# Small products of a modulation vector and of a block merge, streamed with 128 columns instead of 1 and 32

## The chip, the cores and the metric

The kernel runs on one core of a Trainium2 chip. The metric is the device time of one execution in microseconds (us); less is better. Before the change three runs gave 1183.56, 1184.01 and 1186.36 us, median 1184.01.

## The reference

One residual block of a streaming encoder on a sequence of 1024 tokens of width 1024, all in float32:

```python
mod = (c_act @ w_ada[l] + b_ada[l])[:, None, :]          # c_act = silu(c), one vector
shift1, scale1, gate1, shift2, scale2, gate2 = jnp.split(mod, 6, axis=-1)
h = rms_norm(x, norm1_w[l]) * (1.0 + scale1) + shift1
x = x + gate1 * hybrid_mixer(h, ...)     # p = h @ w_in; gated delta rule + short conv; @ w_out
h = rms_norm(x, norm2_w[l]) * (1.0 + scale2) + shift2
x = x + gate2 * swiglu(h, ...)
return rms_norm(x, norm_f_w)
```

Two pieces matter here. The first is the product of the vector `c_act` with the first two column blocks of `w_ada`, which gives `shift1` and `scale1`. The second lies in the gated delta rule: for each head and each chunk of 64 tokens a unit lower triangular 64x64 matrix `lmat` is inverted (`tmat`), and `u = tmat @ v_beta` and `w = tmat @ (k_beta * exp(g))` follow.

## The kernel before, in words

TensorE multiplies 128x128 weights (loaded by a LDWEIGHTS record) with a moving operand of up to 512 columns into one of eight PSUM banks of 128x512. The dense projections split float32 operands into two parts of type float32r and multiply these (128x512 products, one record each; in the profile `acc`, `dn`, `o`). Smaller products take plain float32 operands, and each such product appears as two records, each with a weight load of its own.

The first half of the program (to about 480 us) is not issued in the order in which it is written. Tasks run as threads under a planner (`Sim`, line 298), which keeps an estimated clock for each engine, picks the next operation by priority and estimated start, and so writes out a fixed order for each engine; `Sim.either` (line 438) makes the call, so nearly every operation of this half has line 442 in the profile. Each engine then runs its own list strictly in order and waits on semaphores. The planner's price of a float32 product is `max(n * 0.00168, 0.224)` us for `n` columns (in `Sim.cost`), so 1, 32 and 128 columns all cost it 0.224.

The stages that the change touches:

- Start (to about 54 us). PE first multiplies `ones` by `ident` a number of times into a bank called `heat` whose content nobody reads (line 240 and `acc0`, line 679). `ada0` (line 625) forms `shift1` and `scale1` for eight groups `k` of 128 channels, in one bank (`ada`). Weights are the 128x128 blocks of `w_ada`, and the moving operand is one column of `c_act`. The result of a product is one column, two columns for each group. `sums0` on VectorE (DVE) has summed up most blocks of groups 1 to 7 beforehand, into `ac`; for these a product of `ac` with a column of `ones` does the sum over partitions. `cols0` (line 646, ScalarE, ACT) reads the two columns and makes from them the scale and shift of that group (`s1c`, `b1c`), which `h_make` uses. There are 38 products, 76 records.
- The merge of the delta rule, once for each half of the sequence (`hf` 0 at 202 us, `hf` 1 at 390 us). DVE solves the 32x32 diagonal blocks by substitution (in `gdn`, line 1218); they go to DRAM and come back as `DD`, `xbd` and `XA`. For each of four heads `merge` (line 1178) multiplies twice with 32 moving columns: `P` = weights `L` times a 32-column block of `DD`; ACT copies `P` back into `DD`; `Q` = weights `XA` times that. Four copies of 32x64 place `Q` into `Tt`, the inverse of the 64x64 blocks. Then come the products `u` (weights `Tt`, 128 moving columns) and `w` (128 columns). For each half there are 8 products `P` and 8 `Q`, that is 16 records each. PE's list has all `P`, one `acc` record, all `Q`, and then `u` and `w` with single `acc` records between them.

`bc1(row, n)` (line 140) gives a view with an axis of `n` repeats and step 0; `tsl(t)` (line 1074) is the slice of columns `128*t` to `128*t+128`; `v3(ap, a)` views columns as `a` groups; `mm` (line 581) is one matmul.

Of the kernel before, what the change touches and what calls it, by code (L numbers as in the profile page):

```python
# [12 lines left out]
AF = mybir.ActivationFunctionType  # L13
# [4 lines left out]
P = 128  # L18
# [5 lines left out]
KB = 8  # L24
# [29 lines left out]
def kernel(  # L54
# [25 lines left out]
    class Ordered:  # L80
# [18 lines left out]
    PE, DVE, ACT, POOL, SP = (Ordered(n, e) for n, e in (  # L99
        ("pe", nc.tensor), ("dve", nc.vector), ("act", nc.scalar), ("pool", nc.gpsimd), ("sp", nc.sync)))  # L100
# [30 lines left out]
    def v3(ap, a):  # L131
        return ap.rearrange("p (a b) -> p a b", a=a)

    def flat(ap):
        return ap.rearrange("p a b -> p (a b)")

    def bc2(col, n):
        return col.unsqueeze(2).to_broadcast([col.shape[0], col.shape[1], n])

    def bc1(row, n):  # L140
        return row.unsqueeze(1).to_broadcast([row.shape[0], n, row.shape[1]])
# [10 lines left out]
    ones = ones_r.bitcast(F32)  # L152
# [82 lines left out]
    c_act = cst.tile([P, KB], F32, name="c_act", tag="c_act")  # L235
# [13 lines left out]
    n1c, bac, n2c, gnc = cols_a[:, 0:8], cols_a[:, 8:56], cols_a[:, 56:64], cols_a[:, 64:65]  # L249
    s1c = cst.tile([P, KB], F32, name="s1c", tag="s1c")  # L250
    b1c = cst.tile([P, KB], F32, name="b1c", tag="b1c")
    nb1 = sp.tile([P, KB], F32, name="nb1", tag="nb1")
# [45 lines left out]
    class Sim:  # L298
# [18 lines left out]
        def free(self, t):  # L317
            res, i = self.owner.pop(t.tensor.name)
            res.slots.append((max([a[4] for a in self.acc.get(t.tensor.name, [])] + [0.0]), i))
            res.slots.sort()  # L320
# [238 lines left out]
    def bank(res, name):  # L559
        return res.tile(psp, [P, HT], F32, name)  # L560

    def gt(tag, shape=(P, 4, P), dtype=F32):
        return GP[tag].tile(gp, list(shape), dtype, tag)
# [6 lines left out]
    def ecopy(dst, src):  # L570
        sim.either([("act", "copy", nc.scalar.copy, (dst, src), {}), ("dve", "tensor_copy", nc.vector.tensor_copy, (dst, src), {})])
# [9 lines left out]
    def mm(out_, lhsT, rhs, start=True, stop=True):  # L581
        PE.matmul(out_, lhsT, rhs, start=start, stop=stop)
# [28 lines left out]
    acs_ = {}  # L611
# [13 lines left out]
    def ada0():  # L625
        pa_ = bank(chb, "ada")
        for k in range(KB):
            sim.wait(lambda: ("wa", k) in done)
            t = wa[k]
            pa = pa_[:, 2 * k:2 * k + 2]  # L630
            sim.wait(lambda: k == 0 or k in acs_)
            n0 = KB - N_PE[k]
            for s_ in range(2):
                for kk in range(n0, KB):
                    mm(pa[:, s_:s_ + 1], t[:, kk, s_, :], c_act[:, kk:kk + 1], kk == n0, n0 == 0 and kk == KB - 1)
                if n0:
                    mm(pa[:, s_:s_ + 1], acs_[k][:, s_, :], ones[:, 0:1], n0 == KB, True)
            free(t)
            if n0:
                free(acs_[k])  # L640
            sim.spawn(cols0, PR["ada0"], k, pa)
        sim.wait(lambda: all(("cols", k) in done for k in range(KB)))
        free(pa_)
        done.add("ada0")

    def cols0(k, pa):
        ACT.activation(s1c[:, k:k + 1], pa[:, 1:2], AF.Identity, bias=nb1[:, k:k + 1], scale=n1c[:, k:k + 1])
        ACT.activation(b1c[:, k:k + 1], pa[:, 0:1], AF.Identity, bias=bac[:, k:k + 1])
        done.add(("cols", k))

# [423 lines left out]
    tsl = lambda t: slice(t * P, (t + 1) * P)  # L1074
# [103 lines left out]
    def merge(hf, h, T, XA, DD):  # L1178
        st, t_ = sc_[hf], T[h]
        u = us[hf]  # L1180
        L = t_["L"]
        sim.wait(lambda: ("a", hf, h) in done)
        pP = bank(chb, "P")
        for g in range(2):
            mm(pP[:, 32 * g:32 * g + 32], L[:, 2 * g + 1, :], DD[:, 1, 2 * h + g, :])
        ecopy(DD[:, 0, 2 * h:2 * h + 2, :], v3(pP[:, 0:64], 2))
        free(pP)
        Tt = gt("Tt")
        DVE.transpose(flat(Tt), flat(xbd[0][:, 4 * h:4 * h + 4, :]))
        pQ = bank(chb, "Q")  # L1190
        for g in range(2):
            mm(pQ[:, 32 * g:32 * g + 32], XA[:, 2 * h + g, :], DD[:, 0, 2 * h + g, :])
        for p in range(2):
            for c in range(2):
                q = 64 * c + 32 - 32 * p
                ecopy(Tt[64 * c:64 * c + 32, p:4:2, 64 * c + 32:64 * c + 64], v3(pQ[q:q + 32, 0:64], 2))
        free(pQ)
        done.add(("q", hf, h))
        DVE.tensor_tensor(t_["L"], t_["kt"], bc2(t_["bk"], P), ALU.mult)
        free(t_["bk"])  # L1200
        sim.wait(lambda: ("vt", hf, h) in done)
        pu = bank(chb, "u")
        for t in range(4):
            mm(pu[:, tsl(t)], Tt[:, t, :], u[:, h, t, :])
        ecopy(flat(u[:, h]), pu)
        free(pu)
        pw = bank(chb, "w")
        for t in range(4):
            mm(pw[:, tsl(t)], t_["L"][:, t, :], Tt[:, t, :])
        free(t_["L"])  # L1210
        free(Tt)
        ecopy(t_["WQ"].rearrange("p t (c n) -> p t c n", c=4)[:, :, 0:4:3, :],
                 pw.rearrange("p (t c n) -> p t c n", t=4, c=2))
        free(pw)
        DVE.tensor_tensor(t_["kt"], t_["kt"], bc2(st["kd"][:, :, h], P), ALU.mult)
        done.add(("uw", hf, h))

    def gdn(hf):
# [44 lines left out]
        for h in heads:  # L1263
            sim.spawn(merge, PR["m"], hf, h, T, XA, DD)
# [208 lines left out]
    for f, key in ((load0, "load0"), (load_w, "loadw"), (ada0, "ada0"), (sums0, "sums0"), (xh0, "h0"), (wsplit0, "w0"), (acc0, "acc")):  # L1473
        sim.spawn(f, PR[key])
# [710 lines left out]
```

## Time and profile before

| | |
|---|---|
| median of three runs | 1184.01 us (1183.56 to 1186.36) |
| the profiled execution | 1185.35 us |
| its span, first to last instruction | 1183.6 us (1.75 us lie around it) |
| PE busy, weight loads busy | 1171.5 us, 982.9 us |
| DVE busy, ACT busy | 924.8 us, 536.3 us |
| mean granted clock of TensorE | 0.993 |
| records of `ada` with one column, `P`, `Q` | 76, 32, 32 |

How it is read: a record of PE lasts until its result is written, which is longer than the distance to the next record, because records overlap. What a record costs a row of others is the distance between starts. The chain of waits gives this: it walks back from the last instruction, and a piece of it with `x16` is 16 records one behind the other with the time they took together. "PEclk" in the windows is the clock granted to TensorE as a share of the full one, averaged over the window.

### The profile page before, as it was taken

The numbers are of one execution on the slowest core, as the hardware profiler recorded it, in microseconds if no ns is written. First come the engines' busy times: TensorE is split into PE (matmuls) and PEld (weight loads), VectorE is DVE, ScalarE is ACT, GpSimd is POOL, SyncE is SP. The second block draws the span as 40 slices with busy tenths as digits, with TensorE's granted clock in tenths as the row PEclk, the third lists the DMA queues.
The fourth block names the chain that finished last, engine by engine and source line by source line (L and its number), as shares of the span: only waits on it lengthen the run. The fifth ranks groups of instructions, "written<-read, shape, count | busy, mean of one in ns | idle before, by whom it ended". The sixth has DMA issues, their size and how long they took to land.

```text
span 1183.6 us, 16666 instructions
## 1 busy us (share of the span) xinstructions
PE 1171.5 (99%) x5657; PEld 982.9 (83%) x5657; DVE 924.8 (78%) x1720; ACT 536.3 (45%) x1174; POOL 57.3 (5%) x92
## 2 busy tenths in 40 slices
PE   8999999999999999999999999999999999999997
PEld 8888888988888888888888888888888888888886
DVE  5998888799988798758787677767767697688676
ACT  4489832458642444225443333333333365433343
POOL 2010000001100001100000000000000000000002
PEclk9999999999999899999999999999999999999999
DMA  9932456544434643722354655455644679869413
GB/s 295 291 95 64 112 161 165 177 117 136 119 103 138 158 149 140 280 86 93 133 175 133 222 190 185 145 178 187 223 152 136 221 278 395 307 202 345 146 42 142
DMA packets 179694, 207.58 MB, mean 175 GB/s; under 512 B 25749, under 2 KB 111898, under 8 KB 179610
## 3 DMA queue, kind: packets, MB, share of 16 engines
q1 hardware_dynamic: 172664, 203.16, 53.4%
q10 hardware_dynamic: 6946, 3.38, 1.1%
q8 instruction: 44, 0.72, 0.2%
q14 instruction: 40, 0.33, 0.1%
HBM read 151.44 MB, written 55.05 MB: 174 GB/s over the span
## 4 chain that ended last, share of the span: by engine, by line
PE 93%; DVE 4%; ACT 1%; DMA 1%; issue 1%; POOL 0%; ACTq 0%; DVEq 0%; POOLq 0%
PE acc L91 34%; PE acc L442 24%; PE dn L91 17%; PE o L91 4%; PE o L442 3%; PE K L442 1%; PE A L442 1%; PE u L442 1%; PE ada L442 1%; PE w L442 1%; DVE xo L92 1%; PE ab L442 1%; PE qk L442 1%; PE kk L442 1%; PE heat L91 1%
## 5 line engine op out<-in xcount | busy, mean ns | idle before, releaser
L442 PE MATMUL acc<-h,u 128*128 128x512 f32 x1200 | 303.4, 400 | 0.0
L442 PEld LDWEIGHTS acc<-h,u 128*128 128x128 f32 x1200 | 220.5, 189 | 41.8
L91 PE MATMUL acc<-h,hl 128*128 128x512 f32 x600 | 140.1, 390 | 0.0
L91 PEld LDWEIGHTS acc<-h,hl 128*128 128x128 f32 x600 | 112.4, 188 | 23.2
L91 PE MATMUL acc<-h,u 128*128 128x512 f32 x456 | 106.1, 389 | 0.0
L91 PE MATMUL acc<-T,hl 128*128 128x512 f32 x432 | 101.3, 390 | 0.2 <-ACT cc L92 0.2
L91 PEld LDWEIGHTS acc<-h,u 128*128 128x128 f32 x456 | 85.6, 188 | 17.8
L91 PEld LDWEIGHTS acc<-T,hl 128*128 128x128 f32 x432 | 80.9, 188 | 17.2 <-ACT cc L92 0.6
L92 DVE TENSOR_TENSOR xo<-xo,dn 128x512 f32<-128x512 f32 x84 | 57.1, 685 | 43.2 <-PE dn L91 34.8
L91 PE MATMUL dn<-h,h 128*128 128x512 f32 x396 | 90.7, 389 | 0.0
L92 ACT COPY cc<-acc 128x512 f32<-128x512 f32 x66 | 38.5, 591 | 108.1 <-PE acc L91 108.1
L91 PEld LDWEIGHTS dn<-h,h 128*128 128x128 f32 x396 | 74.3, 188 | 15.4
L91 PE MATMUL acc<-T,u 128*128 128x512 f32 x360 | 84.0, 389 | 0.0
L91 PEld LDWEIGHTS acc<-T,u 128*128 128x128 f32 x360 | 67.6, 188 | 14.0
L442 ACT CAST u<-raw 128x512 fp32r<-128x512 f32 x68 | 42.1, 621 | 57.0 <-PE acc L442 54.9
L92 DVE TENSOR_TENSOR cc<-cc,acc 128x512 f32<-128x512 f32 x66 | 43.8, 683 | 29.8 <-PE acc L91 29.8
L92 DVE TENSOR_TENSOR hl<-R,hl 128x512 fp32r<-128x512 f32 x60 | 39.5, 688 | 33.5 <-ACT hl L92 33.4
L442 DVE TENSOR_TENSOR u<-raw,u 128x512 fp32r<-128x512 f32 x82 | 56.2, 685 | 10.5 <-ACT u L442 10.0
L442 DVE SCALAR_TENSOR_TENSOR cv<-pr,cols_b,cv 128x512 f32<-128x512 f32 x72 | 53.0, 746 | 0.5 <-ACT cv L442 0.2
L92 ACT CAST h<-rw 128x512 fp32r<-128x512 f32 x57 | 32.7, 617 | 39.8 <-PE dn L91 34.6
L92 ACT CAST hl<-R 128x512 fp32r<-128x512 f32 x60 | 35.5, 620 | 24.0 <-DVE R L92 11.0
L92 DVE TENSOR_TENSOR u<-R,u 128x512 fp32r<-128x512 f32 x46 | 30.1, 687 | 20.5 <-ACT u L92 20.5
(344 smaller groups left out, 2020.7 us busy)
## 6 DMA issues: line engine op xcount, KB each, us to landing
raw<-in_w_in_dram SPq DMA_DIRECT2D x82, 256.0 KB, 3.4
am_scr<-cc SPq DMA_DIRECT2D x77, 256.0 KB, 4.4
raw<-in_w_ada_dram SPq DMA_DIRECT2D x56, 256.0 KB, 3.5
rw<-am_scr SPq DMA_DIRECT2D x55, 256.0 KB, 5.3
rw<-bm_scr SPq DMA_DIRECT2D x53, 256.0 KB, 5.3
bm_scr<-raw SPq DMA_DIRECT2D x51, 256.0 KB, 5.4
R<-in_w_gate_dram SPq DMA_DIRECT2D x22, 512.0 KB, 4.1
R<-in_w_up_dram SPq DMA_DIRECT2D x22, 512.0 KB, 5.4
```

The costliest lines, as they stand in the source:

```text
L91: return call(*a, **k)
L92: ins = call(*a, **k)
L442: ins = call(*a, **k)
```

## The change

In `ada0` the moving operand becomes the same column repeated 128 times by an axis of step 0 (`to_broadcast`), and all 128 columns of `ones`. The result is 128 equal columns, in one of two areas of 256 columns of the bank that groups `k` use in turn; `cols0` reads one column of each half of that area. In `merge` the 32-column block becomes four repeats of itself (`bc1(..., 4)`), so each product writes 128 columns; the second product of a pair starts at column 32 and writes over the repeats of the first, and what is read afterwards (columns 0 to 63) is what it was.

```diff
--- ada0
-            pa = pa_[:, 2 * k:2 * k + 2]
+            pa = pa_[:, k % 2 * 256:k % 2 * 256 + 256]
...
-                    mm(pa[:, s_:s_ + 1], t[:, kk, s_, :], c_act[:, kk:kk + 1], kk == n0, n0 == 0 and kk == KB - 1)
+                    mm(pa[:, tsl(s_)], t[:, kk, s_, :], c_act[:, kk:kk + 1].to_broadcast([P, P]), kk == n0, n0 == 0 and kk == KB - 1)
...
-                    mm(pa[:, s_:s_ + 1], acs_[k][:, s_, :], ones[:, 0:1], n0 == KB, True)
+                    mm(pa[:, tsl(s_)], acs_[k][:, s_, :], ones, n0 == KB, True)
--- cols0
-        ACT.activation(s1c[:, k:k + 1], pa[:, 1:2], AF.Identity, bias=nb1[:, k:k + 1], scale=n1c[:, k:k + 1])
+        ACT.activation(s1c[:, k:k + 1], pa[:, P:P + 1], AF.Identity, bias=nb1[:, k:k + 1], scale=n1c[:, k:k + 1])
--- merge
-            mm(pP[:, 32 * g:32 * g + 32], L[:, 2 * g + 1, :], DD[:, 1, 2 * h + g, :])
+            mm(v3(pP[:, 32 * g:32 * g + P], 4), L[:, 2 * g + 1, :], bc1(DD[:, 1, 2 * h + g, :], 4))
...
-            mm(pQ[:, 32 * g:32 * g + 32], XA[:, 2 * h + g, :], DD[:, 0, 2 * h + g, :])
+            mm(v3(pQ[:, 32 * g:32 * g + P], 4), XA[:, 2 * h + g, :], bc1(DD[:, 0, 2 * h + g, :], 4))
```

The lists of the engines keep their length and their order. DVE, ACT, POOL and SP have the same rows as before. On PE the rows of `ada`, `P` and `Q` stand where they stood and differ in their columns. This is PE's list at the merge of the first half, with the rows of before marked - and those of the change marked + (`qs` is the buffer of `DD`, `A` that of `XA`):

```order
 L442 MATMUL acc_2229<-h_0_94_622,u_2125 128x512 x2
-L442 MATMUL P_2274<-qs_2209,L_1196 128x32 x2
-L442 MATMUL P_2275<-qs_2209,L_1197 128x32 x2
-L442 MATMUL P_2276<-qs_2209,L_1198 128x32 x2
-L442 MATMUL P_2277<-qs_2209,L_1199 128x32 x2
+L442 MATMUL P_2274<-qs_2209,L_1196 128x128 x2
+L442 MATMUL P_2275<-qs_2209,L_1197 128x128 x2
+L442 MATMUL P_2276<-qs_2209,L_1198 128x128 x2
+L442 MATMUL P_2277<-qs_2209,L_1199 128x128 x2
 L442 MATMUL acc_2229<-h_0_94_622,u_2125 128x512
```

Nothing moved: the two products of each head keep their place between the same `acc` rows, and only 128x32 became 128x128.

## The prediction, made before the changed kernel ran

> **What bounds the kernel now.** I read the page first, then the chain of waits around the two merges, then windows of 0.2 us for the clock. From the page, the shares of the chain that ended last, and the granted clock in 40 slices of 29.6 us:
>
> ```profile
> PE 93%; DVE 4%; ACT 1%; DMA 1%; issue 1%; POOL 0%; ACTq 0%; DVEq 0%; POOLq 0%
> PEclk9999999999999899999999999999999999999999
> ```
>
> The end is set by PE: 93% of the chain is PE running record behind record. What shortens PE's list shortens the program, as long as nothing else becomes late. And in one slice the clock is below nine tenths. In windows of 0.2 us the slow stretches have sharp edges. The columns are the window, its length, busy time of PE, weight loads, DVE, ACT and POOL, then PEclk, DMA share and GB/s:
>
> ```profile
> 205.40:205.60 0.20, 0.20 (x4) 0.20 (x4) 0.20 (x1) 0.19 (x2) 0.00 (x0) 0.96 0.00 0
> 212.40:212.60 0.20, 0.20 (x3) 0.20 (x3) 0.20 (x1) 0.20 (x1) 0.00 (x0) 0.97 0.76 256
> 393.20:393.40 0.20, 0.20 (x4) 0.20 (x3) 0.20 (x2) 0.20 (x1) 0.00 (x0) 0.80 0.86 279
> 400.00:400.20 0.20, 0.20 (x4) 0.20 (x2) 0.07 (x1) 0.09 (x1) 0.00 (x0) 0.64 0.00 0
> ...
> 209.00:209.20 0.20, 0.20 (x2) 0.20 (x2) 0.20 (x2) 0.00 (x0) 0.00 (x0) 0.50 0.46 154
> ```
>
> Between the edges the clock is 0.50, elsewhere 1.00. A window at 0.96 has spent 0.08 of itself at half clock, so the first stretch begins at 205.58; in the same way it ends at 212.41, and the second runs from 393.32 to 400.14. Both last 6.83 us, and both begin in the middle of `Q`.
>
> The chain of waits through the first one (start, duration, what):
>
> ```profile
> 202.51 1.70 PE P L442 x16
> 204.22 0.31 PE acc L442
> 204.53 2.17 PE Q L442 x16
> 206.69 0.59 PE acc L442
> 207.28 0.43 PE u L442 x2
> 207.71 0.43 PE acc L442
> 208.13 1.71 PE u L442 x8
> 209.84 0.43 PE acc L442
> 210.27 1.71 PE w L442 x8
> 211.97 1.39 PE u L442 x10
> 213.36 0.89 PE w L442 x8
> ...
> 217.85 2.31 PE acc L442 x10
> ```
>
> Eight `w` records take 1.71 us at half clock and 0.89 at full. So at full clock a float32 record of 128 columns costs 0.89 / 8 = 111 ns, an `acc` record 2.31 / 10 = 0.23 us, one of 32 columns (`P`) 1.70 / 16 = 106 ns. The second stretch:
>
> ```profile
> 392.64 1.88 PE Q L442 x12
> 394.53 0.59 PE acc L442
> 395.11 0.69 PE Q L442 x4
> 395.81 1.01 PE acc L442 x2
> 396.82 0.43 PE u L442 x2
> 397.25 0.43 PE acc L442
> 397.67 2.56 PE u L442 x12
> ```
>
> **Why the clock falls there.** These windows of 3.41 us (half of 6.83) are the last one before the first fall, the one after the second rise, and one at the start that has many one-column records:
>
> ```profile
> 202.17:205.58 3.41, 3.41 (x31) 3.33 (x29) 3.29 (x6) 1.46 (x7) 0.00 (x0) 1.00 0.71 224
> 400.15:403.56 3.41, 3.41 (x33) 3.41 (x32) 2.63 (x5) 2.18 (x5) 0.00 (x0) 1.00 0.41 135
> 14.43:17.85 3.42, 2.97 (x27) 2.78 (x26) 2.47 (x4) 1.81 (x4) 0.00 (x0) 1.00 1.16 316
> ```
>
> In the first two, PE and its weight loads are busy throughout, with nearly as many records (31 and 33). One holds `P` and `Q` with 32 columns, and the clock falls behind it. The other holds `u` and `w` with 128 columns, and the clock stays. What differs is how many columns are streamed. If a column costs 0.23 us / 512 = 0.45 ns, a 32-column record streams for 14 of its 106 ns and a 128-column one for 58 of 111. The change makes `P` and `Q` like `u` and `w` in this.
>
> [...]
>
> **What the change removes.** If the clock stays up, the work inside the stretches runs at the full-clock prices above.
>
> First stretch, 6.83 us. Of `Q`, 1.05 us had passed, about 9.9 records at 106 ns; 6.1 remain at 111 ns, 0.68. Then `acc` 0.31 (as the one at 204.22, also behind float32 records), two `u` 0.22, `acc` 0.23, eight `u` 0.89, `acc` 0.23, eight `w` 0.89, and two of the ten `u` 0.23. The sum is 3.68, so 3.15 us go.
>
> Second stretch, from 393.32 to the end of the last `u` at 400.23, 6.91 us. 5.6 `Q` remain of the twelve, 0.62; `acc` 0.31; four `Q` 0.44; two `acc` 0.46; two `u` 0.22; `acc` 0.23; twelve `u` 1.33. The sum is 3.61, so 3.30 us go. Together 6.45.
>
> **What it adds.** Records, waits, and the lists of the other engines stay. Each widened record may take longer. At the start the chain has:
>
> ```profile
> 10.88 1.45 PE heat L442 x12
> 12.54 3.26 PE ada L442 x30
> ```
>
> Thirty one-column records take 109 ns each, `P` 106, and the 128-column records 111 (`w`) to 121 (`heat`, with a change of kind in it). So a record pays hardly for its columns; I take 111. `P` and `Q` are 64 records at +5 ns, 0.32 us; `ada` 76 at +2.6 ns, 0.20 us, counted in full although some lies beside DVE's sums. The lower end of this cost is nothing, since 106 and 111 may be one price. What the trace does not show is a moving operand read through an axis of step 0. The nearest row has weights read so, one column repeated 128 times:
>
> ```profile
> L442 PEld LDWEIGHTS gbc<-qs,row_h 128*128 128x128 f32 x8 | 1.5, 188 | 0.3
> ```
>
> 188 ns is what the plain weight loads of `acc` take as well (188 to 189). I take no cost for it. The upper end is a product that costs as much as one of 512 columns, 0.23 us (see the rivals).
>
> Two areas used in turn mean that group `k` of `ada` overwrites what `cols0` read for group `k-2`. That read is off the path: groups lie several us apart, and PE's list shows no new wait on ACT there.
>
> **What is late next.** PE is earlier by 3.15 us behind the first merge only if DVE and ACT keep up. Between `Q` and `u` stand ACT's copies into `Tt`:
>
> ```profile
> 204.93 3.07 ACT L442 COPY Tt<-Q 32x64 f32<-32x64 f32 x14 [0.46 <-PE Q L442]
> ```
>
> Four copies for a head, 0.22 us each, are ready at 205.8, 206.7 and 207.6 for the first three heads. At full clock PE reaches `u` of the first head at 206.6 (204.53 + 16 x 0.111 + 0.31) and of the second at 207.7, so PE does not wait. Behind that, DVE's waits are what it can give back:
>
> ```profile
> 220.16 0.69 DVE L442 TENSOR_TENSOR u<-raw,u 128x512 fp32r<-128x512 f32 x1 [2.37 <-ACT u L442]
> 221.79 0.69 DVE L442 TENSOR_TENSOR diag<-ada,ident 128x512 f32<-128x512 f32 x1 [0.94 <-PE ada L442]
> ...
> 400.13 1.29 DVE L442 TENSOR_TENSOR h<-raw,h 128x512 fp32r<-128x512 f32 x2 [0.90 <-ACT h L442]
> 402.80 0.69 DVE L442 TENSOR_TENSOR h<-raw,h 128x512 fp32r<-128x512 f32 x1 [0.78 <-ACT h L442]
> 405.68 0.43 DVE L442 CAST u<-raw 128x512 fp32r<-128x512 f32 x1 [1.58 <-PE acc L442]
> ```
>
> 2.37 + 0.94 = 3.31 us behind the first stretch, 0.90 + 0.78 + 1.58 = 3.26 behind the second, nearly all behind PE's work. That is as much as PE gains, with nothing to spare: some tenths may be lost. From 212 to 380 us the chain is PE alone, so what is gained at the first merge should reach the second.
>
> **The sum.** 6.45 - 0.52 = 5.93 us off the profiled execution's 1185.35, 1179.4. That execution was 1.34 above the median of the three runs and inside their range; I take half of that off, **1178.8 us**.
>
> **The rivals.**
>
> 1. One stretch stays, or DVE keeps half of the gain. Before `P` of the second merge PE waits:
>
> ```profile
> 390.36 1.97 PE L442 MATMUL P<-qs,L 128*128 128x32 f32 x16 [1.54 <-DVE ch L442]
> ```
>
> A window that holds this wait streams less than one of `u` and `w`. Against it: with 128 columns the window 389.91 to 393.32 would stream for over 40% of its time. Time: 1178.8 + 3.1 = 1181.9. Chance 0.16.
>
> 2. The columns do not decide. The window 14.43 to 17.85 is the evidence: it has 1.4 us of one-column records and PE is idle for 0.45 us of it, and yet the following rows run at full pace. By columns it streams about 0.7 us (twelve `heat` records), no more than the window before the first fall (0.23 x 2 for `acc` and 26 x 0.014, 0.8 us). So something else may weigh in, such as zeros: `XA` and `L` are mostly zero. Then the clock falls as before and only the 0.52 us come: 1184.01 + 0.4 = 1184.4. [...] If only idleness counted, wider products would change nothing; but PE's row for 202.17 to 205.58 has no idle time at all. Chance 0.15.
>
> 3. The moving stream sets the pace of a record after all, and each of the 98 widened records on the path (64, and about 34 of `ada` behind 25 us, before which DVE's sums are later anyway) pays some 30 ns, half of the 0.45 x 128 ns that its columns stream: 2.9 us of the 6.45 are lost, 1181.8. The rows speak against it (109, 106, 111 ns). [...] Chance 0.03.
>
> 4. The slower one: the step-0 axis is read slowly by the moving port, and a widened record costs what a 512-column one costs, 0.23 instead of 0.11. 98 records at +0.12 are 11.8 us against 6.45 gained: 1184.0 + 5.3 = 1189.3. It decides from 66 ns more for each record (6.45 / 98). Against it stands only the weight load above. Chance 0.06.
>
> **How the numbers follow.** The forecast has 0.60; its own range is 1177.0 (the lowest run less 6.45) to 1180.4. The range of 8 in 10 takes in rivals 1, 2 and 3: 1176.6 to 1184.8. About 0.3% is what a measurement of this kernel can tell from no change, here 1180.46 and 1187.56. Faster beyond that: nine tenths of the forecast and a little of rivals 1 and 3, 0.57. Slower: most of rival 4, 0.05. Within: 0.38.
>
> **What would show it.** PEclk 1.00 in every window from 200 to 215 and from 385 to 405, and `u` and `w` eight records in 0.89 us throughout. `P` and `Q` at about 111 ns in the chain, `ada` too; at 140 or more, rival 3, at 230, rival 4. If a window at 0.50 is left behind `Q`, rival 1 or 2. If the clock is full and the span has lost less than 5 us, new idle time of PE before an `acc` or `o` that waits on DVE would show where it went. The forecast is wrong if the fall of the clock was not due to the columns, or if DVE has less to give back than its waits say.

## The result, and the profile after

| | before | with the change |
|---|---|---|
| median | 1184.00 us (6 runs, 1181.99 to 1186.36) | 1180.22 us (6 runs, 1178.60 to 1181.26) |
| profiled execution, span | 1185.35, 1183.6 us | 1179.96, 1178.2 us |
| mean granted clock | 0.993 | 0.999 |

The ratio is 0.9965, with a 95% interval of 0.9952 to 0.9979. The kernel became 3.8 us faster, a little more than the 0.3% that a measurement can tell; the forecast was 5.2 us.

The page after, the granted clock in 40 slices; the slice below nine tenths is gone:

```profile
PEclk9999999999999999999999999999999999999999
```

The stretches of both merges in windows (window, length, busy time of PE, weight loads, DVE, ACT, POOL, then PEclk, DMA share, GB/s):

```profile
200.00:215.00 15.00, 15.00 (x117) 14.24 (x115) 12.91 (x22) 7.92 (x27) 1.48 (x2) 1.00 0.71 189
386.00:406.00 20.00, 17.71 (x135) 16.69 (x135) 17.22 (x30) 14.16 (x38) 0.95 (x1) 1.00 0.59 176
```

PEclk is 1.00 in both. The chain through the first merge after the change:

```profile
203.05 1.78 PE P L442 x16
204.84 0.24 PE acc L442
205.07 1.78 PE Q L442 x16
206.86 0.23 PE acc L442
207.09 0.22 PE u L442 x2
207.31 0.24 PE acc L442
207.55 0.89 PE u L442 x8
208.44 0.23 PE acc L442
208.68 0.89 PE w L442 x8
209.57 1.12 PE u L442 x10
...
214.27 0.89 PE w L442 x8
```

Every float32 record now takes 1.78 / 16 = 111 ns, `P` and `Q` too. From the start of `P` to the end of the last `w` it is 215.16 - 203.05 = 12.11 us, where before it was 217.85 - 202.51 = 15.34: 3.23 us less. The second merge:

```profile
388.39 2.04 PE P L442 x16
390.44 0.23 PE acc L442
390.67 1.34 PE Q L442 x12
392.01 0.23 PE acc L442
392.24 0.44 PE Q L442 x4
...
400.34 0.89 PE w L442 x8
```

From the start of `P` to the end of the last `w` it is 401.23 - 388.39 = 12.84 us. Before, the chain had here:

```profile
390.37 1.97 PE P L442 x16
...
405.64 0.89 PE w L442 x8
```

That is 406.53 - 390.37 = 16.16 us, so 3.32 us less with the change.

### The profile page after: what moved, and what is told of

Same layout as the page of the kernel before. It is cut to its first block, busy times and chain, and to the rows that moved or that the text cites. A ratio compares the mean times of both kernels' runs of the same rounds, so it can differ in the third digit from the quotient of the medians.

```text
span 1178.2 us, 16667 instructions
## 1 busy us (share of the span) xinstructions
PE 1165.3 (99%) x5657; PEld 977.4 (83%) x5657; DVE 924.9 (79%) x1720; ACT 536.3 (46%) x1174; POOL 57.9 (5%) x92
## 4 chain that ended last, share of the span: by engine, by line
PE 92%; DVE 4%; DMA 2%; SPq 1%; ACT 1%; issue 1%; ACTq 0%; DVEq 0%
PE acc L91 34%; PE acc L442 24%; PE dn L91 17%; PE o L91 4%; PE o L442 3%; SPq L442 1%; PE K L442 1%; PE A L442 1%; DVE xo L92 1%; PE ab L442 1%; PE w L442 1%; PE u L442 1%; PE qk L442 1%; PE kk L442 1%; PE ada L442 1%
```

## The experiments

The theory was that the few streamed columns of `P` and `Q` let the clock fall, and that wider products keep it up. The rivals were that the columns do not decide, that one merge alone matters, that DVE or the reloads take the gain back, and that a streamed column has a price of its own.

The expectations below speak of free windows of 3.413 us. The length is read from the profile of before: its two stretches begin 187.74 us apart (205.58 and 393.32), 55 times 3.413, and each lasts twice that. A window is such a length, counted from the edges of a profile; free says that its place in the program differs from one execution to another, which was an assumption until the profiles before_b to before_d.

### Which part of the change does it

**P and Q alone widened.** The edit is the change without its lines in `ada0` and `cols0`:

```diff
-            mm(pP[:, 32 * g:32 * g + 32], L[:, 2 * g + 1, :], DD[:, 1, 2 * h + g, :])
+            mm(v3(pP[:, 32 * g:32 * g + P], 4), L[:, 2 * g + 1, :], bc1(DD[:, 1, 2 * h + g, :], 4))
...
-            mm(pQ[:, 32 * g:32 * g + 32], XA[:, 2 * h + g, :], DD[:, 0, 2 * h + g, :])
+            mm(v3(pQ[:, 32 * g:32 * g + P], 4), XA[:, 2 * h + g, :], bc1(DD[:, 0, 2 * h + g, :], 4))
```

> Only P and Q are widened, the modulation products stay at one column. Theory (the columns of P and Q keep the clock up, and ada is nearly free either way): PEclk 1.00 behind both merges, time within 1 us of the changed kernel, about 1180. Rival (the ada half matters, either as a cost of its wider records or as a guard of the clock in the start): as a cost, this kernel is 0.5 to 2 us faster than the changed one; as a guard, PEclk falls to 0.50 somewhere before 30 us in the profile or the median lies 1 to 3 us above the changed kernel.

Measured: 1179.62 us, ratio 0.9958 (0.9945 to 0.9971); the clock holds in both merges of its profile and in the start (PEclk 1.00 in 200 to 215, 386 to 406 and 14 to 20). As far as can be told, the whole gain lies in the merges. Against the changed kernel no difference can be told, since the two intervals overlap. Three of the six runs had a mean clock of 0.995 to 0.998, where the profiled one had 0.999, so slow stretches are left in some executions; these have no profile that would show where.

**The modulation products alone widened** (the areas of the bank and `cols0` as in the change, `P` and `Q` at 32 columns).

```diff
-                    mm(pa[:, s_:s_ + 1], t[:, kk, s_, :], c_act[:, kk:kk + 1], kk == n0, n0 == 0 and kk == KB - 1)
+                    mm(pa[:, tsl(s_)], t[:, kk, s_, :], c_act[:, kk:kk + 1].to_broadcast([P, P]), kk == n0, n0 == 0 and kk == KB - 1)
...
-                    mm(pa[:, s_:s_ + 1], acs_[k][:, s_, :], ones[:, 0:1], n0 == KB, True)
+                    mm(pa[:, tsl(s_)], acs_[k][:, s_, :], ones, n0 == KB, True)
```

> Only the modulation products are widened, P and Q keep 32 columns. Theory: both stretches of half clock stay, time as before or 0.2 to 0.5 us above, about 1184. Rival (ada contributes to the gain): 1 us or more below before.

Measured: 1184.24 us, ratio 1.0001 (0.9990 to 1.0011). No gain of its own that can be told. But in its profile the slow stretches were not where they had been: one of 3.41 us from 206.52 and one of 10.24 us from 390.84.

**One merge at a time**, with `ada` at one column (the second kernel has `hf == 1`):

```diff
-            mm(pP[:, 32 * g:32 * g + 32], L[:, 2 * g + 1, :], DD[:, 1, 2 * h + g, :])
+            if hf == 0:
+                mm(v3(pP[:, 32 * g:32 * g + P], 4), L[:, 2 * g + 1, :], bc1(DD[:, 1, 2 * h + g, :], 4))
+            else:
+                mm(pP[:, 32 * g:32 * g + 32], L[:, 2 * g + 1, :], DD[:, 1, 2 * h + g, :])
```

(and the same for `Q`)

> P and Q are widened in the merge of the first half of the sequence alone, ada stays at one column. Theory (each merge pays for its own slow stretch): the stretch behind 205 us goes, the one behind 390 us stays where the free windows allow it, and about half of the gain comes, 1.5 to 3 us below before. Rival (what the first merge gains is lost again in the wait for the reloads before the second P): less than 1 us, and PE's idle time before the second P is up by over 2 us.

> P and Q are widened in the merge of the second half alone, ada stays at one column. Theory: the stretch behind 205 us stays, the one behind 390 us goes, 1.5 to 3 us below before, so that this and the kernel with the first merge alone add up to the kernel with both. Rival (DVE, saturated from 418 to 440 us, keeps what the second merge gains): less than 1 us below before, with new idle time of PE at 440 us.

Measured: the first merge alone 1184.36 us, ratio 0.9995 (0.9985 to 1.0005); the second alone 1181.86 us, ratio 0.9966 (0.9952 to 0.9980). The first merge alone brings nothing that can be told: its median lies 0.3 us above that of before beside it (1184.09), its ratio 0.6 us below. So its theory (1.5 to 3 us) failed, and its rival (the wait before the second `P` takes the gain back) falls too: PE's wait there was 1.6 us against 1.5 before, not 2 us more. The second has its stretch behind 205 us and none behind 390, and brings 2.2 us by the medians, as its theory had it, and 4.0 us by the ratio (interval 2.4 to 5.7). By the ratios the two add up to 4.6 us, where `P` and `Q` of both bring 5.0. The profile of the kernel with the first merge alone shows what happened:

```profile
15.00:16.00 1.00, 1.00 (x7) 1.00 (x7) 1.00 (x2) 0.00 (x0) 0.00 (x0) 0.54 1.26 303
21.00:22.00 1.00, 1.00 (x4) 0.81 (x3) 0.94 (x3) 0.00 (x0) 0.00 (x0) 0.55 1.10 353
200.00:215.00 15.00, 15.00 (x111) 14.04 (x110) 13.73 (x23) 7.70 (x27) 1.68 (x3) 1.00 0.73 191
390.00:391.00 1.00, 1.00 (x9) 1.00 (x8) 1.00 (x2) 0.91 (x3) 0.00 (x0) 0.77 0.89 303
400.00:401.00 1.00, 1.00 (x7) 1.00 (x7) 0.49 (x1) 0.48 (x1) 0.00 (x0) 0.61 0.00 0
```

The first merge is at full clock, but there is a slow stretch from 15.08 to 21.90 inside the one-column products of the start, which the profile of before did not have, and the one of the second merge is 10.24 us long instead of 6.83. That the clock held in the first merge says nothing for the columns here, since it held there with 32 columns too in the three profiles that follow (PEclk 1.00 in 205 to 206 in each).

### Where the slow stretches lie

So the kernel before was profiled three more times, unchanged.

> The kernel before, once more, for its profile alone. Theory (free windows): the slow stretches begin at another place in the program than 205.58 and 393.32 us, both shifted alike modulo 3.413 us, and last one, two or three windows; the time follows the sum of their lengths. Rival (the fall belongs to a fixed instruction): both begin within 0.1 us of the same records of Q and last 6.83 us again.

> As before_b, a further profile of the kernel before. Theory: yet another place of the windows; where a window lies wholly inside the one-column products of the start, a third stretch appears there. Rival: the same two stretches at the same records.

> As before_b, a further profile of the kernel before. Theory: the first merge loses less than the second in the mean, since its stretch can be one window short or absent, while PE's wait before the second P makes the second one longer. Rival: both merges lose 3 us each in every profile.

Measured: 1186.64, 1184.87 and 1182.14 us. The edges in the first of these three:

```profile
15.00:16.00 1.00, 1.00 (x9) 1.00 (x9) 1.00 (x2) 0.00 (x0) 0.00 (x0) 0.81 1.27 305
22.00:23.00 1.00, 1.00 (x5) 0.79 (x4) 1.00 (x3) 0.00 (x0) 0.00 (x0) 0.78 1.14 336
205.00:206.00 1.00, 1.00 (x13) 1.00 (x11) 0.94 (x2) 0.36 (x2) 0.00 (x0) 1.00 0.90 208
391.00:392.00 1.00, 1.00 (x7) 1.00 (x6) 1.00 (x3) 0.80 (x3) 0.00 (x0) 0.54 0.88 312
401.00:402.00 1.00, 1.00 (x9) 1.00 (x9) 0.28 (x1) 0.69 (x2) 0.00 (x0) 0.84 0.00 0
```

It falls at 15.62 for 6.83 us and at 391.09 for 10.24 us, and not at all in the first merge. In the third one:

```profile
205.00:206.00 1.00, 1.00 (x11) 1.00 (x11) 1.00 (x3) 0.92 (x6) 0.00 (x0) 1.00 0.01 4
389.00:390.00 1.00, 1.00 (x7) 0.94 (x6) 1.00 (x2) 1.00 (x3) 0.00 (x0) 0.57 0.90 271
395.00:396.00 1.00, 1.00 (x6) 1.00 (x5) 1.00 (x3) 0.00 (x0) 0.00 (x0) 0.51 0.00 0
396.00:397.00 1.00, 1.00 (x11) 1.00 (x10) 0.47 (x1) 0.67 (x2) 0.00 (x0) 1.00 0.00 0
```

only the second merge falls. The rival of a fixed instruction is out. The theory for the last of the three held: the first merge loses less than the second. Taken together, with the length of the slow stretches in us, each read from such windows:

| profile | start | first merge | second merge | sum | time, us |
|---|---|---|---|---|---|
| before | 0 | 6.83 | 6.83 | 13.66 | 1185.35 |
| before_b | 6.83 | 0 | 10.24 | 17.07 | 1186.64 |
| before_c | 3.41 | 0 | 10.24 | 13.65 | 1184.87 |
| before_d | 0 | 0 | 6.83 | 6.83 | 1182.14 |
| ada alone widened | 0 | 3.41 | 10.24 | 13.65 | 1186.41 |
| first merge alone | 6.83 | 0 | 10.24 | 17.07 | 1185.70 |
| second merge alone | 0 | 6.83 | 0 | 6.83 | 1182.51 |
| P and Q alone | 0 | 0 | 0 | 0 | 1178.71 |
| the changed kernel | 0 | 0 | 0 | 0 | 1179.96 |

Not counted are the beginning and the end of the program. The trace's record of the clock starts at 7.6 us in the profile of before and at 8.3 in that of the changed kernel, at full clock; the `heat` records ahead of that are slow (4 in the half microsecond from 3.00 of before, 7 in that from 8.50). At the end the clock is at 0.50 for the last 1.8 us of before and the last 2.5 of the changed kernel, in which no record of PE runs. Every length in the table is one, two or three times 3.413 us, and inside a profile the beginnings lie whole windows apart (391.09 - 15.62 = 110 x 3.413). Where the windows begin differs from execution to execution: 205.58 and 15.62 are 0.8 and 2.0 us behind a multiple of 3.413. And the time follows the sum: from before_d to before_b it is 4.50 us for 10.24 us more at half clock, 0.44 us for each, about the half that is lost. The runs without a profile agree: of 59 runs of the kernel before that stand beside the experiments, the seven with the highest mean clock (0.996) took 1181.68 to 1182.65 us, and the 20 with 0.992 took 1183.69 to 1187.41.

This explains the single merges. Of the six profiles above whose first merge had 32 columns three fell there, 2.8 us in the mean, which at 0.47 (3.23 / 6.83) costs 1.3 us; the kernel with the first merge alone gained 0.6 by its ratio (interval from a loss of 0.6 to 1.8). All six with a 32-column second merge fell there, 9.1 us in the mean, which costs 4.3 us; the kernel with the second alone gained 4.0 by its ratio.

In the first merge it can also be compared at a like place of the windows. In the three profiles that fell there, a window begins between 0.34 us before and 0.17 us behind the start of `P`. In three profiles with 128 columns (the changed kernel twice, `P` and `Q` alone) one begins between 0.41 before and 0.21 behind, and the clock holds.

### How many columns it takes, and what one costs

The same edit with another number of repeats, `ada` at one column; here 64 columns:

```diff
-            mm(pP[:, 32 * g:32 * g + 32], L[:, 2 * g + 1, :], DD[:, 1, 2 * h + g, :])
+            mm(v3(pP[:, 32 * g:32 * g + 64], 2), L[:, 2 * g + 1, :], bc1(DD[:, 1, 2 * h + g, :], 2))
```

(and the same for `Q`)

For 256 columns the repeats are 8 and the planner's price of such a product is held at 0.224, so that the lists of the engines stay as they are:

```diff
-                    busy = max(n * 0.000443, 0.107) if fast else max(n * 0.00168, 0.224)
+                    busy = max(n * 0.000443, 0.107) if fast else 0.224 if n == 256 else max(n * 0.00168, 0.224)
```

> P and Q stream 256 columns (eight repeats), ada keeps one column. Theory (the weight loads set the pace of a record until its columns need longer than they do): 256 columns stream for 115 ns, so a record takes 112 to 125 ns instead of 111 and the time is 0 to 1 us above the kernel with 128. Rival (a repeated axis is read slowly, hidden at 128): 180 ns or more for each record, 4 us or more above.

Measured: 1186.46 us, ratio 1.0018 (1.0008 to 1.0028), although the clock holds in both merges (PEclk 1.00 in 200 to 222 and 390 to 410; its profile has one slow stretch, 6.83 us in the start). The chain through its first merge:

```profile
204.71 3.45 PE P L442 x16
208.17 0.23 PE acc L442
208.39 3.45 PE Q L442 x16
...
213.66 0.89 PE w L442 x8
```

A record of 256 columns takes 3.45 / 16 = 216 ns, 0.84 ns a column, against 0.45 for the float32r records of `acc`. The theory for this run was wrong: its 0.45 ns a column belongs to another kind of operand. The rival as written, an axis that is read slowly, does not follow either: at 0.84 ns 128 columns take 108 of the 111 ns that `w` takes too, whose operand has no repeats. A plain operand of 256 columns was not run. For the 64 records the 216 instead of 111 ns are 6.7 us; the medians differ by 6.8 (1186.46 and 1179.62, measured beside different runs of before).

So the shares of the prediction were too low. Estimated at 0.84 ns a column, a 32-column record streams for 27 of 106 ns (25%), one of 64 for 54 (51%), one of 96 for 81, and one of 128 for 108 of 111.

> P and Q stream 64 columns instead of 32 (two repeats), ada keeps one column. If a window falls by the share of its time in which columns stream (0.8 us of 3.41, 24%, in the window before the first fall; about 48% in a window of u and w, which holds), 64 columns give about 35% there, and the kernel tells on which side the limit lies: at or below 35%, as the kernel with P and Q at 128, about 1180; above it, as before, about 1184. Rival (an own cost of each streamed column): no fall of the clock and yet no gain.

Measured: 1184.76 us, ratio 0.9996 (0.9983 to 1.0008). Its profile had no fall in either merge, only 3.41 us in the start, but was with 1180.63 us the fastest of 12 runs (to 1186.86). The runs fall into two groups: five with a mean clock of 0.996, the profiled one among them, took 1180.63 to 1182.67 us, seven with 0.992 or 0.993 took 1183.73 to 1186.86. So the profile shows the lesser part of the runs, and one more of the same kernel was taken.

> The kernel with 64 columns once more, for a profile with the windows at another place. Revised theory (a float32 record streams at 216 / 256 = 0.84 ns a column, so 64 columns fill about half of a record's 106 ns and 32 a quarter): no fall in the first merge, where PE has no wait; a fall behind the second merge where a window holds both the wait before P and most of P. Rival (64 columns hold the clock everywhere and the median of 1184.8 has another cause): no fall in either merge, and about 1184.

Measured: 1184.03 us, with these windows and this row of PE:

```profile
200.00:215.00 15.00, 15.00 (x117) 14.24 (x116) 13.23 (x22) 7.97 (x28) 1.47 (x2) 1.00 0.74 192
387.93:391.34 3.41, 2.25 (x18) 1.97 (x18) 3.41 (x7) 1.78 (x6) 0.00 (x0) 1.00 0.88 248
391.00:392.00 1.00, 0.73 (x4) 0.76 (x5) 1.00 (x3) 1.00 (x3) 0.00 (x0) 0.67 0.53 196
398.00:399.00 1.00, 1.00 (x10) 1.00 (x10) 0.42 (x1) 0.63 (x2) 0.00 (x0) 0.92 0.00 0
391.27 2.09 PE L442 MATMUL Q<-qs,A 128*128 128x64 f32 x9 [1.16 <-DMA A<-dx]
```

The second merge falls for 6.83 us (391.35 to 398.18), as the theory had it, but by another wait than the one it named. PE's wait of 1.6 us before `P` ended at 387.82, in front of the window that comes before the fall. That window holds `P` and 1.16 us of waiting for the reload of `XA` before `Q`, so half-filled records fill only about a third of it (by the estimate 16 x 54 ns for `P` and 0.23 us for an `acc`, 1.1 of 3.41 us). In the first profile of this kernel PE did not wait between `P` and `Q`, and the clock held. That the first merge held in both profiles does not show that 64 columns are enough there: a window began 1.0 and 1.7 us behind the start of `P`, and with 32 columns the clock held where one began 1.3 us behind it (before_c).

> P and Q stream 96 columns (three repeats), ada keeps one column. Revised theory: 96 columns fill 81 of about 108 ns, the windows of both merges hold, and the time is that of the kernel with 128 columns and a narrow ada, 1179.5 to 1181. Rival (only a record that is full of columns holds the clock in the second merge, with its wait): a fall of 3.4 us or more behind the second P and a median of 1182 or more.

Measured: 1181.08 us, ratio 0.9963 (0.9950 to 0.9976), no slow stretch in its profile, which took 1179.22 us. 96 columns are enough in both merges of that profile, whose windows lie as where 32 columns fell (one begins 0.23 us before the first `P`). Its other five runs had a mean clock of 0.995 to 0.997 and no profile; where they were slow is open, and its `ada` has one column.

The two profiles of the main comparison can be read window by window. Take for each window of 3.413 us the share of it in which columns stream, each record's counted from its start, at 0.84 ns a column for plain float32 and 0.45 for float32r. This share is an estimate from the two prices measured above (216 ns for 256 columns, 0.23 us for 512). In the profile of before it is 34% ahead of the first fall (202.17 to 205.58) and 26% ahead of the second (389.91 to 393.32). The lowest shares behind which the clock stayed at 1.00 are 39% (11.02 to 14.43) and 44% (14.43 to 17.85, the window of rival 2). In the profile of the changed kernel the lowest such share is 58% (387.14 to 390.55). So in the profile of before the clock fell in the start and the merges behind the two lowest shares, once after a wait (PE busy for 2.96 of 3.41 us ahead of the second fall) and once after thin records without a pause (3.41 of 3.41 ahead of the first). With 0.45 ns for every column, as the prediction had it, the order does not hold: 24% ahead of the first fall, but 21% in 11.02 to 14.43, behind which the clock stayed up. How low a share the clock bears in other kernels is not shown.

### The changed kernel again

> The changed kernel once more, with more runs, beside the two kernels below. Theory (the time of a run depends on where the free windows of 3.413 us lie, and the widened products take that dependence away): median 1179.5 to 1180.5, a spread of runs of 3 us or less against 4 to 5 us for the kernel before, and PEclk 1.00 behind both merges and in the start. Rival (the spread has another source, such as the transfers): the spread is as wide as that of the kernel before.

Measured: 1180.04 us, ratio 0.9959 (0.9946 to 0.9973), PEclk 1.00 in the start and both merges. The six runs lie within 1.3 us (1179.15 to 1180.42; the six of the result within 2.7), 23 runs of the kernel before beside them within 4.5 (1182.65 to 1187.17). The spread goes with the slow stretches, as expected.

This profile also shows what the `ada` half does. Its 32 `heat` records at the beginning were slow for long (6.79 us), as in before_b (6.68; 6.18 in the first profile of before), which means that the windows lie nearly alike in the two. PE in before_b, one column:

```profile
12.99 4.01 PE L442 MATMUL ada<-c_act,wa 128*128 128x1 f32 x30
17.33 2.77 PE L442 MATMUL heat<-ident,ones 128*128 128x128 f32 x12
20.60 2.70 PE L442 MATMUL acc<-h,whl 128*128 128x512 f32 x7
```

and in the changed kernel:

```profile
13.12 3.51 PE L442 MATMUL ada<-c_act,wa 128*128 128x128 f32 x30
16.69 1.50 PE L442 MATMUL heat<-ident,ones 128*128 128x128 f32 x12
19.30 1.88 PE L442 MATMUL acc<-h,whl 128*128 128x512 f32 x7
```

With one column the clock falls at 15.62 and the `heat` records behind take 2.77 us instead of 1.50. The transpose `pt` that closes the start begins at 55.49 instead of 56.97. Eleven profiles had the one-column products, with a fall in the start in six of them; three had the wide ones, with none. The place of the windows is not what makes this difference. In the six that fell the windows lie 1.4 to 3.3 us behind a multiple of 3.413, in the other five 0.0 to 0.8; in the three wide ones they lie 1.5 to 2.2 behind, where one column fell (1.4 with the first merge alone, 2.0 in before_b).

## Why the prediction was right or wrong

**The columns keep the clock up: right.** Both stretches are gone, at places of the windows where 32 columns fell. `P` to the end of `w` shortened by 3.23 and 3.32 us, 6.55 together, with the cost of the wider records in it; the prediction had 6.45 less 0.32, that is 6.13.

**The price of a widened record: right for the kernel, wrong in its reason.** 111 ns, as taken. But a float32 column costs 0.84 ns and not 0.45, so 128 columns just about fill the 106 to 109 ns that a record takes with 32 columns or 1, and do not stream for half of it, as the prediction had it. That the change stops at 128 was luck in this respect: by 0.45 ns 256 columns would have been nearly free as well, and they cost 6.8 us. The 0.84 ns also takes away rival 2's evidence: the window 14.43 to 17.85 streamed 14 x 108 ns = 1.5 us (`heat`, and two transposes of 128 columns), more than the window before the first fall (0.46 for two `acc`, and 26 x 27 ns, together 1.2). That more columns are enough, with the zeros of `L` and `XA` unchanged, is shown, and the start fell with blocks of `w_ada` as weights, which the reference fills with random numbers. Rival 4 did not come: the repeats cost no more than `w`'s own columns (111 ns a record in both).

**What is late next: right.** DVE and ACT kept up behind both merges. Of what the first merge gained, 0.7 us did not reach the second `P`, because PE waited 2.3 us there instead of 1.5. Since that wait was between 1.5 and 2.2 us in the four profiles of before, it is not shown that the change makes it longer.

**`ada` as a cost of 0.20 us: the wrong kind of term.** Thirty records take 3.36 instead of 3.26 us, which is the size forecast. But in about half of the profiles the one-column products let the clock fall in the start, and the change prevents that, 1.5 us where the windows lie as in before_b. (A second pair, the kernel with the first merge alone and the first profile of the changed one, has `pt` at 56.65 and 55.01.) Whether this outweighs its cost in the median is open.

**The sum: the step that failed is the last one**, "I take half of that off". Against its own profiled execution the sum was 1179.4, and the changed kernel measured 1180.22 and 1180.04, so without that step it would have been off by 0.6 to 0.8 us and not by 1.2 to 1.4. Its profiled execution took 0.54 us longer to reach the first `P`, with `heat` slow for longer and `ada` wider; that and the 0.7 above make up the difference between 6.55 gained in the merges and 5.4 in the span, to 0.1. The profile of before had 13.66 us at half clock, while other executions had between 6.83 and 17.07. The changed kernel has none in the start and the merges of its two profiles, and 11 of its 12 runs had a mean clock of 0.998 or 0.999, so its time had nothing to do with where that execution stood among the runs of before. The prediction took no account of windows that lie elsewhere in each execution (0.8 us behind a multiple of 3.413 in the profile of before, 2.0 in before_b): the stretches of one profile are one draw, and the gain is their mean. It was luck that the profiled execution stood near it: the four profiles of before have 12.8 us in the mean. (Two rivals' times are a tenth of a microsecond off their own terms: 1184.01 + 0.52 is 1184.5, 1178.8 + 2.9 is 1181.7.)

## What to carry to other kernels

Here the granted clock went to 0.50 behind 3.41 us of small products in which PE was busy throughout, so look at the granted clock in narrow windows wherever products have few columns. Filling the records up to the time that they take even with one column (here 128 float32 columns, 111 ns against 106 to 109) was nearly free, and beyond that the columns were paid (216 ns for 256). What went with the falls of this kernel is the share of a window in which columns stream (34% and 26% in the profile of before), so a wait beside thin records made it worse: the 26% is the window with 0.45 us of idle PE. Where a loss differs from execution to execution, as the time at half clock does here (6.83 to 17.07 us in four profiles of before), take several profiles before you size it, and size it by the mean.

## What the runs showed of the hardware that was not expected

A plain float32 record streams at 0.84 ns a column (216 ns for 256), a float32r record at 0.45 (0.23 us for 512). The slow stretches in the start and the merges lasted 3.41, 6.83 or 10.24 us. In the profile of before they begin behind the windows with the lowest estimated share of streaming columns (34% and 26%; 39% and more where the clock stayed up), the first of them although PE had no idle time there (202.17 to 205.58 us, busy 3.41 of 3.41). One of the first six runs of the changed kernel had a mean clock of 0.997 where the other five had 0.999, and took 1181.26 us; it has no profile, so whether a stretch remained there, and where, stays open.
